# Layer 0 in three passes over the tokens: u first, then linear attention beside the state-space scan, then gates, half GLU and output projection

## The chip, the cores and the metric

The kernel runs on one core of a Trainium2 chip. The time is that of one launch in device microseconds (us). Profiled durations come from one execution that the hardware profiler recorded; engines are named as in the profile: PE (TensorE matmuls), PEld (its weight loads), DVE (VectorE), ACT (ScalarE), POOL (GpSimd), SP (SyncE, which issues the DMAs).

## What is computed

Two layers over a prompt of 4096 tokens of width 1024, and over a sample of 8 x 4 tokens that shares the weights. Layer 0 is the one that changes:

```
proj = rms_norm(x, g) @ w_in            # 1024 -> 512+512+256+256+512+16+512
u, gate_a, q, k, v, a_low, gate_b = split(proj)
y, s5_last = s5_scan(u, ...)            # 32 groups of 16 channels, one 64-dim complex diagonal state each, over all tokens
z = gelu(y); z = z * sigmoid(z @ w_glu + b_glu)          # half GLU
out_a = z * silu(gate_a)
log_a = log_sigmoid(a_low @ w_gate + b_gate) / 16
o, gla_last = gla_chunked(q, k, v, log_a, s0)            # 4 heads, chunks of 64
out_b = rms_norm(o, g) * silu(gate_b)
h = x + concat(out_a, out_b) @ w_out    # 1024 -> 1024
```

Layer 1 (projection, rotary, sliding-window attention with sinks, gate, projection) stays as it is.

## The kernel before

Tokens are taken in 16 windows of 256. Every product with a weight is made of three f16 matmuls (high by high, low by high, high by low parts), so x is first multiplied by its norm's factor (`x <- x,rb`, L312 on DVE), rounded (`xh`, L313 on ACT) and the rest taken (`xl`, L314 on POOL). Weights are split in the same way (L244, L245), each after a bound on its size was summed over its squares (`bound_all`, L212 on DVE).

Work is written as generators that yield costs. `merge` takes the next piece from the stream that is furthest behind its weight, and so sets the order of the instructions on each engine; every engine then runs its own list strictly in order.

`phase0` merges three streams. `ustream` projects u of window after window and writes it to DRAM. `s5stream` first builds the scan's tables for all 32 groups and then runs `s5win` as soon as u of four windows is there. `bounds` sums squares of weights. A unit of the scan is 4 groups by 1024 tokens, laid out as 128 positions of 8 tokens; there are 32 units, eight per call of `s5win`. A unit has 12 fp32 matmuls of 128x128 on PE (`pV`, L768; `pY`, L785 and L788), and between them on DVE a multiply (L773), a rotation (L746 to L750), four recurrences (L777), a multiply (L780), a second rotation, and two small copies (L779, L782). For the last eight units some of these operations are on POOL:

```
RO = ('vvvdv', 'vggdg')
merge((ustream(), 170.0), (s5stream(), SW), (bounds(), BW))
```

`phase1` runs window by window. `instream(w)` holds gate_a (`ga`), gate_b with the gate code (`gb`), q and k, v; `bstream(w)` holds the half GLU (`glu`), the chunked linear attention (`core`, whose first DVE operation in a window is `attm`, L1095) and the output projection (`outstream`, L1346 adds its result to x):

```
merge((bstream(w), 35.0), (instream(w + 1), 50.0), side)
```

The side stream holds the bounds of layer 1's weights in windows 0 to 6 and the sample in windows 7 to 9. The last eight units of the scan are run beside the loading of layer 0's weights, and layer 1's weights are loaded in the tail of `phase1`. Three PSUM banks (`pmm`) take the products of `phase1`.

`phase2` is layer 1.

Of the kernel before, what the change touches and what calls it, by code (L numbers as in the profile page):

```python
# [19 lines left out]
KT = 8  # L20
# [11 lines left out]
TW, SW, BW, HP, HS, HT, LW, SMP1 = 0.3, 100.0, 60.0, 100000, 0, 0, 27.0, 9  # L32
LW2 = 30.0
OB, WG = 2, 28
VQ = (0, 1)
GL, CA, CB = 0, 3.0, 40.0
# [3 lines left out]
EA, ST1 = 15, 12  # L40
RO = ('vvvdv', 'vggdg')
BW0 = 0
BE = 'v'
BG, SMP0, SC = 8.0, 7, 8.0
# [36 lines left out]


class Stage:


    def __init__(self, xp, og):
        self.xp, self.og, self.n = xp, og, 0

    def tile(self, shape, dtype, name):
        self.n += 1  # L90
        if self.n % 2:
            return self.xp.tile([128, 512], F32, name="x")
        a = self.og.tile([128, KT, NW], F16, name="ogh" if self.n % 4 else "ogl")
        return a.rearrange("p k n -> p (k n)").bitcast(F32)[:, 0:512]
# [12 lines left out]
class K:  # L107
# [87 lines left out]
    def bound_all(self, src, blocks, g, nk, name, sp, pp, tag="misc"):  # L195
# [3 lines left out]
        if g is not None and pp is not self.pms:  # L199
            g2 = sp.tile([128, nk], F32, name=name + "_g2")  # L200
            nc.vector.tensor_mul(g2, g, g)
        fr = self.cp.tile([128, len(ch) * nk], F32, name=name + "_fr")
        for i, (_, c, m) in enumerate(ch):
            for k in range(nk):
                st = sp.tile([128, 512], F32, name="wst")
                nc.sync.dma_start(st[:, 0:m], src[128 * k:128 * k + 128, c:c + m])
                a = fr[:, i * nk + k:i * nk + k + 1]
                if pp is self.pms or BE == "a":
                    nc.scalar.activation(st[:, 0:m], st[:, 0:m], AF.Square, bias=0.0,
                                     scale=g[:, k:k + 1] if g is not None else 1.0, accum_out=a)  # L210
                else:
                    (nc.vector if BE == "v" else nc.gpsimd).scalar_tensor_tensor(st[:, 0:m], st[:, 0:m], g2[:, k:k + 1] if g is not None else 1.0, st[:, 0:m],  # L212
                                     op0=OP.mult, op1=OP.mult, accum_out=a)
                yield 1.0
# [59 lines left out]
    def stats(self, acc, n, rst, blk0, wp, pp, tag="misc"):  # L274
# [7 lines left out]
        self.rms(ps, n, rst, blk0, wp)  # L282

    def rms(self, ps, n, rst, blk0, wp):
# [6 lines left out]
        nc.gpsimd.tensor_tensor(rst[0:m, blk0:blk0 + nb], v[0:m, 0:nb], self.mhalf[0:m, 0:nb], op=OP.pow)  # L291

# [12 lines left out]
    def xsplit(self, xs, n, rb, hp):  # L305
# [3 lines left out]
        for x in xs:  # L309
# [59 lines left out]
    def s5_tables(self):  # L369
        nc, I = self.nc, self.I  # L370
        with ExitStack() as e2:
            t = self.pool("s5t", es=e2)
            pp = self.pool("s5p", bufs=2, es=e2, space=PSUM)

            def T(name, *shape):
                return t.tile([128] + list(shape), F32, name=name)

            lam = T("lam", 2, G5)
            nc.sync.dma_start(lam, I["lam"])
            ld = t.tile([G5, 1], F32, name="ld")  # L380
            nc.sync.dma_start(ld, I["log_dt"])
            bc = T("bc", 4, G5, 16)
            nc.sync.dma_start(bc, I["s5_bc"])
            Dd = t.tile([16, G5], F32, name="Dd")
            nc.sync.dma_start(Dd, I["s5_d"])
            lre, lim = lam[:, 0], lam[:, 1]
            B1, B2, P1, P2 = (bc[:, k] for k in range(4))
            ec = T("ec", G5)
            nc.vector.memset(ec, math.e)
            for m in self.Mt:  # L390
                nc.gpsimd.memset(m, 0.0)
            yield 0.1

            dd = t.tile([G5, G5], F32, name="dd")
            nc.gpsimd.tensor_tensor(ld, ec[0:G5, 0:1], ld, op=OP.pow)
            nc.vector.tensor_scalar(dd, self.identf[0:G5, 0:G5], ld, None, op0=OP.mult)
            pd = pp.tile([128, 4, 128], F32, name="pv")
            nc.tensor.matmul(pd[:, 0, 0:G5], self.onesf[0:G5, :], dd, start=True, stop=True)
            dt = T("dt", G5)
            nc.vector.tensor_copy(dt, pd[:, 0, 0:G5])  # L400
            nc.vector.tensor_scalar(lim[0:64], lim[0:64], -1.0, None, op0=OP.mult)
            nc.vector.tensor_scalar(P1[64:128], P1[64:128], -1.0, None, op0=OP.mult)
            nc.vector.tensor_scalar(P2[64:128], P2[64:128], -1.0, None, op0=OP.mult)

            red = T("red", G5)
            nc.vector.tensor_mul(red, lre, dt)
            nc.vector.tensor_scalar(red[64:128], red[64:128], 8.0, None, op0=OP.mult)
            mg = T("mg", G5)
            nc.gpsimd.tensor_tensor(mg, ec, red, op=OP.pow)
            mag = T("mag", G5)  # L410
            for h in range(2):
                r = slice(64 * h, 64 * h + 64)
                nc.vector.tensor_copy(mag[r], mg[0:64])
                nc.vector.tensor_copy(self.r8[r], mg[64:128])

            ang = T("ang", 8, G5)
            nc.vector.tensor_mul(ang[:, 0], lim, dt)
            for j in range(1, 8):
                nc.vector.tensor_scalar(ang[:, j], ang[:, 0], 8.0 * 2.0**(j - 1), None, op0=OP.mult)
            kk = T("kk", 8, G5)  # L420
            nc.vector.tensor_scalar(kk, ang, 1.0 / TWO_PI, MAGIC, op0=OP.mult, op1=OP.add)
            nc.vector.tensor_scalar(kk, kk, MAGIC, None, op0=OP.subtract)
            for c in (C1, C2, C3):
                nc.vector.scalar_tensor_tensor(ang, kk, -c, ang, op0=OP.mult, op1=OP.add)
            nc.vector.tensor_scalar(ang, ang, 3.1415925, -3.1415925, op0=OP.min, op1=OP.max)
            sn, cs = T("sn", 8, G5), T("cs", 8, G5)
            nc.scalar.activation(sn, ang, AF.Sin, bias=0.0, scale=1.0)
            nc.scalar.activation(cs, ang, AF.Sin, bias=0.0, scale=0.5)
            nc.vector.tensor_mul(cs, cs, cs)
            nc.vector.tensor_scalar(cs, cs, -2.0, 1.0, op0=OP.mult, op1=OP.add)  # L430
            yield 1.0

            Lr, Li = self.Lr, self.Li
            nc.vector.memset(Lr[:, 0], 1.0)
            nc.vector.memset(Li[:, 0], 0.0)
            nc.vector.tensor_mul(Lr[:, 1], mag, cs[:, 0])
            nc.vector.tensor_mul(Li[:, 1], mag, sn[:, 0])

            def cmul(orr, oi, ar, ai, br, bi, tmp):
# [393 lines left out]
    def phase1(self, es0, tail):  # L833
# [572 lines left out]
        def some(g, n):  # L1406

            while n > 0:
                c = next(g, None)
                if c is None:  # L1410
                    return
# [738 lines left out]
```

## Time and profile before

| | us |
|---|---|
| three runs | 3288.75, 3296.31, 3296.82 (median 3296.31) |
| profiled execution | 3289.11, of which the span is 3287.3 |
| first u matmul to last u matmul | 14.5 to 403 |
| units of the scan | 195 to 502 |
| first `attm` of window 0, 1, 2 | 516.6, 623.1, 695.0 |
| first `attm` of windows 11 to 15 | 1457.5, 1537.6, 1617.8, 1698.0, 1769.0 |
| end of layer 0's last output projection, first product of layer 1 | 1822.0 |

The stretch up to 516.6 is called the head below, and the time from one window's first `attm` to the next window's a window interval. PE is busy for 3150.1 us, but a matmul's record lasts longer than the distance to the next one, so PE counts as busy while it waits between two of them for less than that.

### The profile page before, as it was taken

How to read it: one execution, taken by the hardware profiler on the slowest of the kernel's cores; microseconds unless marked ns; L12 is line 12 of the kernel's file. 1: busy time of each engine (PE TensorE's matmuls, PEld its weight loads, DVE VectorE, ACT ScalarE, POOL GpSimd, SP SyncE). 2: the span in 40 equal slices, each digit the busy share in tenths (PEclk: the TensorE clock that was granted, in tenths of full speed). 3: DMA queues.
4: the chain of work that ended last, by engine and by line, in shares of the span. 5: the costliest groups of instructions: out<-in, count | busy, mean ns of one | idle time of the engine just before them, and what ended most of it. 6: DMA issues, size and time to landing. Idle time of an engine off the chain costs nothing.

```text
span 3287.3 us, 68398 instructions
## 1 busy us (share of the span) xinstructions
PE 3150.1 (96%) x27293; PEld 2458.2 (75%) x27293; DVE 2054.4 (62%) x4785; ACT 1688.5 (51%) x4054; POOL 1261.2 (38%) x1292
## 2 busy tenths in 40 slices
PE   6898879899999999999999999999999999999999
PEld 5687766687788777788877667777777777777777
DVE  8869998644444443444446477666666666666675
ACT  4386556233344343343345366565555656555664
POOL 7824241211111211111111565554555555555552
PEclk9799989999999999999999999999999999999999
DMA  4297467411111112211113212111111111101111
GB/s 128 60 252 176 95 149 223 121 46 49 46 49 46 44 45 71 58 50 46 43 53 122 72 36 62 41 40 41 36 42 40 34 37 37 34 28 41 40 32 43
DMA packets 329521, 222.79 MB, mean 68 GB/s; under 512 B 142544, under 2 KB 302240, under 8 KB 329056
## 3 DMA queue, kind: packets, MB, share of 16 engines
q1 hardware_dynamic: 329200, 218.41, 24.2%
q8 instruction: 214, 3.51, 0.4%
q14 instruction: 107, 0.88, 0.1%
HBM read 164.94 MB, written 53.23 MB: 66 GB/s over the span
## 4 chain that ended last, share of the span: by engine, by line
PE 75%; DVE 11%; ACT 4%; issue 4%; DMA 4%; POOL 3%; SPq 1%; DVEq 0%; POOLq 0%; ACTq 0%
PE mm L325 13%; PE mm L326 13%; PE mm L327 13%; PE mm L334 7%; PE mm L335 7%; PE mm L336 7%; PE po L1760 3%; PE pt L1718 2%; PE ps L1699 2%; PE ps L1700 2%; PE pt L1568 1%; DVE z L777 1%; POOL xl L314 1%; DVE x L312 1%; DMA wst<-in_w_in 1%
## 5 line engine op out<-in xcount | busy, mean ns | idle before, releaser
L325 PE MATMUL mm<-ogh,woh 128*128 128x256 f16 x1472 | 401.3, 273 | 1.4 <-DVE xr L1346 1.4
L326 PE MATMUL mm<-ogl,woh 128*128 128x256 f16 x1472 | 401.3, 273 | 0.5 <-POOL ogl L1772 0.5
L327 PE MATMUL mm<-ogh,wol 128*128 128x256 f16 x1472 | 401.3, 273 | 0.0
L314 POOL TENSOR_TENSOR xl<-x,xh 128x512 f16<-128x512 f32 (+1 forms) x196 | 261.3, 1355 | 319.1 <-ACT xh L313 306.1
L1683 ACT ACTIVATE Sc<-Sc,ng,rq 128x128 f32<-128x128 f32 x512 | 245.6, 482 | 107.1 <-DVE ng L1677 105.7
L272 POOL TENSOR_TENSOR acc<-acc,sq 128x512 f32<-128x512 f32 x48 | 61.8, 1288 | 565.4 <-issue 370.4
L1711 POOL TENSOR_TENSOR Pl<-Sc,Ph 128x512 f16<-128x512 f32 x128 | 153.3, 1198 | 275.6 <-ACT Ph L1710 244.9
L326 PEld LDWEIGHTS <-woh 128*128 128x128 f16 x2112 | 207.2, 98 | 36.4 <-issue 9.8
L325 PEld LDWEIGHTS <-woh 128*128 128x128 f16 x2112 | 207.2, 98 | 31.6 <-issue 4.6
L336 PEld LDWEIGHTS <-xl 128*128 128x128 f16 x1536 | 151.0, 98 | 106.0 <-issue 6.7
L334 PEld LDWEIGHTS <-xh 128*128 128x128 f16 x1536 | 150.9, 98 | 102.5 <-issue 17.7
L327 PEld LDWEIGHTS <-wol 128*128 128x128 f16 x2112 | 207.1, 98 | 25.5 <-issue 3.1
L335 PEld LDWEIGHTS <-xh 128*128 128x128 f16 x1536 | 151.0, 98 | 84.0 <-issue 5.1
L325 PE MATMUL mm<-xh,wuh 128*128 128x256 f16 (+1 forms) x544 | 151.6, 283 | 14.2 <-ACT us L727 6.9
L313 ACT ACTIVATE xh<-x 128x512 f16<-128x512 f32 (+1 forms) x196 | 117.8, 618 | 75.6 <-DVE x L312 61.7
L326 PE MATMUL mm<-xl,wuh 128*128 128x256 f16 (+1 forms) x544 | 151.4, 284 | 4.9 <-POOL xl L314 4.9
L1720 ACT ACTIVATE PT<-pt 128x1024 f16<-128x1024 f16 x128 | 129.6, 1013 | 42.1 <-PE pt L1718 42.1
L327 PE MATMUL mm<-xh,wul 128*128 128x256 f16 (+1 forms) x544 | 151.1, 283 | 0.0
L312 DVE TENSOR_TENSOR x<-x,rb 128x512 f32<-128x512 f32 (+1 forms) x188 | 136.5, 781 | 22.5 <-ACT rb L302 18.2
L1346 DVE SCALAR_TENSOR_TENSOR xr<-mm,soa,xr 128x512 f32<-128x512 f32 x64 | 47.7, 745 | 160.5 <-PE mm L327 155.8
L326 PE MATMUL mm<-xl,wi1gah 128*128 128x256 f16 x512 | 141.4, 277 | 3.0 <-POOL xl L314 3.0
L327 PE MATMUL mm<-xh,wi1gal 128*128 128x256 f16 x512 | 141.0, 276 | 2.4 <-DVE wi1gal L245 2.4
(730 smaller groups left out, 10558.9 us busy)
## 6 DMA issues: line engine op xcount, KB each, us to landing
x<-in_xT SPq DMA_DIRECT2D x128, 256.0 KB
wst<-in_w_in SPq DMA_DIRECT2D x64, 256.0 KB
xr<-in_xT SPq DMA_DIRECT2D x64, 256.0 KB
h_d<-xr SPq DMA_DIRECT2D x64, 256.0 KB
x<-h_d SPq DMA_DIRECT2D x64, 256.0 KB
xr<-h_d SPq DMA_DIRECT2D x64, 256.0 KB
out_yT<-xr SPq DMA_DIRECT2D x64, 256.0 KB
wst<-in_w_out SPq DMA_DIRECT2D x48, 256.0 KB
```

The lines of the kernel that those rows point to most:

```text
L312: nc.vector.tensor_mul(x, x, rb[:, None, :].to_broadcast([128, 2, n]))
L313: nc.scalar.activation(h, x, AF.Copy, bias=0.0, scale=1.0)
L314: nc.gpsimd.tensor_sub(l, x, h)
L325: nc.tensor.matmul(ps, wh[:, k0 + k, c], xh[k], start=(k == 0), stop=False)
L326: nc.tensor.matmul(ps, wh[:, k0 + k, c], xl[k], start=False, stop=False)
L327: nc.tensor.matmul(ps, wl[:, k0 + k, c], xh[k], start=False, stop=(k == n - 1))
L334: nc.tensor.matmul(ps, xh[k][:, t], wh[:, k, c0:c1], start=(k == 0), stop=False)
L335: nc.tensor.matmul(ps, xh[k][:, t], wl[:, k, c0:c1], start=False, stop=False)
L336: nc.tensor.matmul(ps, xl[k][:, t], wh[:, k, c0:c1], start=False, stop=(k == n - 1))
L1683: nc.scalar.activation(Sc[:, i], Sc[:, i], AF.Exp, bias=ng[:, i:i + 1], scale=scale[:, i:i + 1], accum_out=de[:, i:i + 1])
L1711: nc.gpsimd.tensor_sub(Pl, Sc, Ph)
L1720: nc.scalar.activation(PT, pt.rearrange("p a i n -> p (a i) n"), AF.Copy, bias=0.0, scale=1.0)
```

## The change

Layer 0 is cut into three passes over all tokens, with weights and tables placed to suit.

- Pass A (`phaseA`): u of all 16 windows; the scan's tables for the first two of eight quarters (4 groups each); bounds and splits of the weights of gate_b, q, k and v.
- Pass B (`phaseB`): window by window gate_b, v, q and k of the next window beside the linear attention of this one, and beside them the scan (`some(s, SB)`: pieces of a total weight of 10 per window). The scan goes quarter by quarter, with four units to a quarter, and the tables of quarter q+2 are built after quarter q in one of two buffers. All of a unit's multiplies are on DVE. When the scan is done, the same stream loads the weights of gate_a, half GLU and output. The side stream holds bounds in windows 0 to 6 and the sample in 7 to 9, as before. The norm's factor comes by a broadcast DMA from DRAM (`rbload`) and not by a matmul; the multiply x by rb is on POOL. The halves of x and of the attention's output are written to DRAM.
- Pass C (`phaseC`): the halves come back from DRAM; gate_a and half GLU of the next window beside the output projection of this one, and beside them the splits of layer 1's weights.

Passes A and B have two PSUM banks for products, pass C three. Matmuls on PE go from 25,975 to 25,976; DMAs that SP issues from 1,197 to 1,778.

```
-RO = ('vvvdv', 'vggdg')
+SB, BG, SC = 10.0, 13.0, 8.0
+RO = ("vvvdv", "vvvdv", "vvvdv", "vvvdv")
...
     def xsplit(self, xs, n, rb, hp, mul=None, dst=None):
...
-            nc.vector.tensor_mul(x, x, rb[:, None, :].to_broadcast([128, 2, n]))
+            (mul or nc.vector).tensor_mul(x, x, rb[:, None, :].to_broadcast([128, 2, n]))
             nc.scalar.activation(h, x, AF.Copy, bias=0.0, scale=1.0)
             nc.gpsimd.tensor_sub(l, x, h)
+            if dst is not None:
+                for i, a in enumerate((h, l)):
+                    nc.sync.dma_start(dst[:, i, 2 * c:2 * c + 2], a)
...
+        for q in range(8):                       # s5_units
+            for w in range(4):
+                yield from unit(q, w)            # yields 1.7 and 0.9
+            if q + 2 < 8:
+                yield from self.quarter(q + 2)   # yields 3 x 0.7, 0.5, 1.5, 0.5
...
-        merge((ustream(), 170.0), (s5stream(), SW), (bounds(), BW))
+        merge((ustream(), 170.0), (tables(), 18.0), (loads(), 66.0))     # end of phaseA
...
+        def prep(w):                             # phaseB
+            rb = self.rbload(self.rs0[w], Pb)
+            Ws[w]["x"] = self.xsplit(Ws[w]["x"], n, rb, hp, nc.gpsimd, self.xp_d[w])
...
+        merge((instream(0), 50.0), (self.some(s, SB), SB))
+        for w in range(NWIN):
...
+            merge((core(w), 35.0), (instream(w + 1) if w + 1 < NWIN else None, 50.0), (self.some(s, SB), SB), side)
...
+        run(front(0))                            # phaseC; front = gate_a, half_glu
...
+        for w in range(NWIN - 1):
+            merge((outstream(w), 21.0), (front(w + 1), 17.0), (self.some(wg, 3.0), 3.0),
+                  (self.some(smp, 4.0) if w < 4 else None, 4.0))
```

How the order on two engines moves, at the places that the prediction speaks of. First DVE while u is projected. Before, between the multiplies of one window's x and the next, stand operations of the scan (`X`, `t`, `z`, `carry`):

```order
L780 TENSOR_TENSOR X<-z,CT_109 128x4x128
L743 TENSOR_TENSOR t_3119<-z,ST_110 64x512
L744 TENSOR_TENSOR t_3119<-z,ST_110 64x512
L748 TENSOR_TENSOR t_3841<-t_3841,ST_86 128x512
L773 TENSOR_TENSOR X<-pV,CT_85 128x4x128
L779 COPY X<-carry 128x4
L750 TENSOR_TENSOR X<-X,t_3119 128x4x128
L750 TENSOR_TENSOR X<-X,t_3841 128x4x128
L220 COPY wa_n_4447<-misc 128x1
L312 TENSOR_TENSOR x<-x,rb 128x512 x4
L782 COPY carry<-X 128x4
```

In the change the same multiplies (now at L299) have only the sums of squares between them, once the two quarters' tables are built:

```order
L299 TENSOR_TENSOR x<-x,rb 128x512 x4
L274 TENSOR_SCALAR var<-pt 128x2
L734 TENSOR_TENSOR sq<-sq 128x512
L299 TENSOR_TENSOR x<-x,rb 128x512 x4
L734 TENSOR_TENSOR sq<-sq 128x512
L274 TENSOR_SCALAR var<-pt 128x2
L734 TENSOR_TENSOR sq<-sq 128x512 x2
L299 TENSOR_TENSOR x<-x,rb 128x512 x4
```

The scan's operations have left this stage. They stand in pass B; this is DVE there in the change, in the window in which the sample begins, where `q` and `k` are what empties the banks of products (`mm`) and `X`, `t`, `z` and `carry` are one unit of the scan:

```order
L603 TENSOR_TENSOR X<-X,t_9927 128x4x128
L625 SCALAR_TENSOR_TENSOR z<-r_95,carry,X 128x128 x4
L628 TENSOR_TENSOR X<-z,CT_85 128x4x128
L601 TENSOR_TENSOR t_9927<-z,ST_86 64x512
L602 TENSOR_TENSOR t_9927<-z,ST_86 64x512
L603 TENSOR_TENSOR X<-X,t_9927 128x4x128
L630 COPY carry<-X 128x4
L627 COPY X<-carry 128x4
L943 SCALAR_TENSOR_TENSOR q_10015<-mm,sr_3602,E 128x256
L948 SCALAR_TENSOR_TENSOR k_10016<-mm,sr,E 128x256
```

Here the operations that free a PSUM bank have moved behind most of a unit. Last, POOL in windows after the sample. Before, it held the rests of x (`xl`), the squares of the output (`acc`) and the rest of the half GLU's output (`ol`):

```order
L314 TENSOR_TENSOR xl<-x,xh 128x512 x4
L272 TENSOR_TENSOR acc<-acc,sq 128x512
L277 TENSOR_TENSOR acc<-acc 128x256
L291 TENSOR_TENSOR rst_77<-var,mhalf 128x2
L1058 TENSOR_TENSOR ol<-A,oh 128x512 x2
```

In pass B of the change it holds the multiplies of x, between the rests of x and the head norm's powers (`rs`):

```order
L301 TENSOR_TENSOR xl<-x,xh 128x512 x4
L299 TENSOR_TENSOR x<-x,rb 128x512 x3
L965 TENSOR_TENSOR rs<-ss,mhalf 128x4
L299 TENSOR_TENSOR x<-x,rb 128x512
L965 TENSOR_TENSOR rs<-ss,mhalf 128x4
L301 TENSOR_TENSOR xl<-x,xh 128x512 x4
```

The multiplies have come over from DVE, and the squares and the half GLU have gone to pass C.

## Rows read from the trace of the kernel before

**Rows 1.** The profile page: span, busy time of each engine, DVE in 40 slices.

```profile
span 3287.3 us, 68398 instructions
PE 3150.1 (96%) x27293; PEld 2458.2 (75%) x27293; DVE 2054.4 (62%) x4785; ACT 1688.5 (51%) x4054; POOL 1261.2 (38%) x1292
DVE  8869998644444443444446477666666666666675
```

**Rows 2.** Five stretches: us, busy PE, PEld, DVE, ACT, POOL; clock, DMA share, GB/s.

```profile
0.00:516.60 516.60, 418.63 (x3243) 356.85 (x3244) 458.01 (x893) 306.05 (x621) 253.87 (x187) 0.90 0.58 146
516.60:695.00 178.40, 165.35 (x1321) 130.19 (x1321) 119.56 (x322) 73.62 (x165) 30.33 (x28) 0.97 0.47 141
695.00:1768.90 1073.90, 1066.21 (x8906) 842.50 (x8905) 475.24 (x1217) 430.31 (x1009) 200.21 (x174) 1.00 0.19 52
1768.90:1822.00 53.10, 47.55 (x389) 38.99 (x387) 39.74 (x92) 25.64 (x56) 17.24 (x18) 0.90 0.53 161
1822.00:3287.00 1465.00, 1452.33 (x13442) 1089.69 (x13439) 961.81 (x2264) 852.88 (x2205) 759.54 (x888) 1.00 0.13 39
```

**Rows 3.** Stretches inside the head, columns of rows 2.

```profile
14.50:166.90 152.40, 121.29 (x884) 99.96 (x884) 133.55 (x256) 59.67 (x112) 127.13 (x88) 0.80 0.31 77
166.90:189.20 22.30, 22.30 (x201) 19.78 (x199) 6.63 (x10) 16.92 (x38) 7.31 (x7) 0.97 0.98 255
202.00:403.00 201.00, 175.36 (x1472) 156.51 (x1470) 196.96 (x377) 130.52 (x273) 59.60 (x43) 0.95 0.67 165
195.00:490.00 295.00, 246.57 (x1985) 218.84 (x1986) 286.62 (x538) 187.19 (x388) 100.61 (x72) 0.92 0.66 161
```

**Rows 4.** DVE by line, 195 to 517 us: first and last of the scan's nine groups.

```profile
L777 DVE TENSOR_TENSOR_SCAN z<-r,carry,X 128x128 f32<-128x128 f32 x128 | 62.0, 545 | 0.1
...
L779 DVE COPY X<-carry 128x4 f32<-128x4 f32 x31 | 8.9, 291 | 0.0
```

**Rows 5.** Tables on DVE, 0 to 517 us: first and last of thirteen groups.

```profile
L511 DVE SCALAR_TENSOR_TENSOR Ks<-identf,Dd,Ks 16x16 f32<-16x16 f32 x32 | 13.3, 464 | 0.0
...
L524 DVE TENSOR_TENSOR CT<-CT,cs 128x256 f32<-128x256 f32 x4 | 1.5, 404 | 0.0
```

**Rows 6.** POOL by line, 0 to 517 us.

```profile
L314 POOL TENSOR_TENSOR xl<-x,xh 128x512 f16<-128x512 f32 x71 | 105.2, 1503 | 106.1 <-ACT xh L313 105.9
...
L780 POOL TENSOR_TENSOR X<-z,CT 128x512 f32<-128x512 f32 x8 | 11.2, 1402 | 21.3 <-DVE z L777 18.4 <-DVE wi_gs L238 2.9
```

**Rows 7.** Lines L777, L312 and L314 over the span: ns min/median/max.

```profile
L777 DVE TENSOR_TENSOR_SCAN z<-r,carry,X x128: 448/460/1366, 206.7 to 493.6; 128x128 f32<-128x128 f32 x128
L312 DVE TENSOR_TENSOR x<-x,rb x188: 205/686/1755, 15.3 to 3137.4; 128x512 f32<-128x512 f32 x184, 128x64 f32<-128x64 f32 x4
L314 POOL TENSOR_TENSOR xl<-x,xh x196: 305/1171/4447, 19.7 to 3139.7; 128x512 f16<-128x512 f32 x192, 128x64 f16<-128x64 f32 x4
```

**Rows 8.** Four fp32 matmuls in the timeline (two records each), then an f16 one.

```profile
433.21 1.06 PE L785 MATMUL pY<-U,Mt 128*128 128x128 f32 x8
434.10 0.27 PE L327 MATMUL mm<-xh,wi1gal 128*128 128x256 f16 x1
```

**Rows 9.** One window interval without sample or scan, columns of rows 2.

```profile
1537.60:1617.80 80.20, 80.20 (x667) 64.41 (x665) 35.03 (x86) 31.46 (x74) 15.55 (x14) 1.00 0.18 47
```

**Rows 10.** DVE by line in that interval: one of its groups.

```profile
L1346 DVE SCALAR_TENSOR_TENSOR xr<-mm,sob,xr 128x512 f32<-128x512 f32 x5 | 3.7, 746 | 9.6 <-PE mm L327 9.6
```

**Rows 11.** The three window intervals that hold the sample, columns of rows 2.

```profile
1168.80:1264.00 95.20, 91.17 (x762) 68.48 (x763) 45.21 (x123) 41.03 (x100) 15.93 (x14) 0.98 0.16 42
1264.00:1374.80 110.80, 108.72 (x918) 81.64 (x920) 43.16 (x121) 37.59 (x91) 19.87 (x17) 1.00 0.24 67
1374.80:1457.50 82.70, 82.70 (x699) 66.12 (x692) 33.81 (x90) 32.32 (x75) 15.00 (x15) 1.00 0.19 50
```

**Rows 12.** Chain that ended last: one DMA wait after the head.

```profile
541.76 4.53 DMA wst<-in_w_in
```

**Rows 13.** SP's timeline: one DMA issue.

```profile
1457.56 0.37 SPq L1358 DMA_DIRECT2D h_d<-xr  x1
```

More of the change, by code (lines that the diff above doesn't have):

```diff
@@ new lines, in ustream, with loads, tables @@
+                                nc.sync.dma_start(self.u_d[w][ct][:, :, 64 * (h // 2):64 * (h // 2) + 64], us[:, ct])
+        def loads():
+            yield lambda: self.udone >= 0
+            yield from self.bound_all(I["w_in0"], self.B_IN0, self.g0, KT, "wi1", bp, pms, "pt", ("v", "a"))
+            self.wr["wi1"] = self.pow2(self.bound["wi1"], "wi1")
+            for b in ("v", "gb", "qk"):
+                yield from self.load_w(I["w_in0"], self.SRC[b], self.g0, "wi1", *W1[b], bp)
+        def tables():
+            yield from self.s5_tables()
+            yield from self.quarter(0)
+            yield from self.quarter(1)
@@ L946, in instream @@
             x = W["x"]
-            if w + 1 < NWIN:
-                yield from gate_a(w)
             alT = Pa.tile([16, NW], F32, name="alT")
@@ new lines, in phaseB @@
+        Ws = [{} for _ in range(NWIN)]
+        Ws[0]["x"] = self.xload(xp, I["xT"], 0, n)
+        prep(0)
+        s, bnd, smp = s5(), bounds(), sample()
+        merge((instream(0), 50.0), (self.some(s, SB), SB))
+        for w in range(NWIN):
+            side = (None, 1.0)
+            if w < SMP0:
+                side = (self.some(bnd, BG), BG)
+            elif SMP0 <= w <= SMP1:
+                if w == SMP0:
+                    run(bnd)
+                    eb.close()
+                    self.smp = self.pool("smp1", es=eb, side=R)
+                side = (self.some(smp, SC), SC)
+            merge((core(w), 35.0), (instream(w + 1) if w + 1 < NWIN else None, 50.0), (self.some(s, SB), SB), side)
+            if w == SMP1:
+                run(smp)
+                eb.close()
+            Ws[w] = None
@@ L1406, in some @@
[L1406 to L1411, printed above, removed]
-                yield c
-                n -= 0 if callable(c) else c
-        bnd, smp = bounds(), sample()
-        for w in range(NWIN - 1):
-            side = (None, 1.0)
-            if BW0 <= w < SMP0:
-                side = (some(bnd, BG), BG)
-            elif SMP0 <= w <= SMP1:
-                if w == SMP0:
-                    run(bnd)
-                    eb.close()
-                    self.smp = self.pool("smp1", es=eb)
-                side = (some(smp, SC), SC)
-            merge((bstream(w), 35.0), (instream(w + 1), 50.0), side)
-            if w == SMP1:
+        Ws = [{} for _ in range(NWIN)]
@@ L1454, in weights @@
-        def weights():
-            for b, (c, m) in src.items():
-                yield from self.load_w(I["w_in1"], [(0, c, m)], self.g1, "wi2", *W2[b], st)
-        st = Stage(xp, og2)
-        wg = weights()
-        for _ in range(WG):
-            next(wg)
-        rb = self.rbcast(self.rst1, 0, NW, xp, self.pta, tag="pt", rtag="x")
+        er, el = self.er2, ExitStack()
+        W2 = self.W2
+        hp = self.pool("h2", bufs=4, es=er, side="right")
+        xp = self.pool("x2", bufs=3, es=er, side="right")
```

1202 lines of the change are left out of this document (594 added, 608 removed).

## The prediction

> **What bounds the kernel now.** I read the page first. PE is busy for 96% of the span, so by the average it is the bound; but DVE's slices stand at 8 and 9 in the first six of forty and at 4 in the next eleven [rows 1]. So the stages are looked at apart. Layer 1 is 1465.0 us with PE busy for 1452.3, and the thirteen window intervals from 695 on have PE busy for 1066.2 of 1073.9 [rows 2]: there the change can gain little but by leaving out matmuls, and it leaves out none. In the head DVE is busy for 458.0 of 516.6 us [rows 2], and in the scan, from 195 to 490, for 286.6 of 295.0 while PE shows 246.6 of records that count waits too [rows 3]. That PE waits there is seen in the u projection: where nothing else presses, two windows of u take 22.3 us, all of it PE [rows 3], 11.15 a window; from 202 to 403, with the scan beside, the rest of u goes at about 21 a window with DVE at 197.0 of 201.0 [rows 3]. The head is therefore DVE's, the rest PE's. What lies idle there is DVE: 35.0 of 80.2 us in a plain window interval [rows 9].
>
> **Prices of PE's work.** The 22.3 us hold 201 matmuls [rows 3]: 0.111 each for 128x256 in f16. Four fp32 ones take 0.89 from one row's start to the next [rows 8], 0.223 each; a unit of the scan has 12, so 2.67 us. Gate_a, half GLU and output have 96 + 48 + 192 = 336 matmuls a window, 37.3 us; the plain interval of 80.2 [rows 9] leaves 42.9 for gate_b, v, q, k and the attention. The three intervals with the sample show PE busy for 91.2, 108.7 and 82.7 [rows 11], 42 over three plain ones.
>
> **Pass A, the head up to the first attention.** What leaves it: 28 of 32 units. The first instream runs with 10 of scan beside it, and a unit yields 2.6, so four units start there. PE's work in the new head is 16 x 11.15 = 178.4 for u, 42.9 for the first instream, 10.7 for four units, and some 30 for norm sums, table matmuls of two quarters and bounds (an estimate without a row of its own): 262. DVE loses 28/32 of the scan's nine groups, which sum to 229.6 [rows 4], so 200.9, and 6/8 of the tables' thirteen, which sum to 66.3 [rows 5], so 49.7; 458.0 becomes 207, below PE. How well PE is fed is bounded by two stretches: 121.3 of 152.4 (0.80) where the tables are built beside u, and 22.3 of 22.3 after them [rows 3]. With the start at 14.5 these give 14.5 + 262/0.80 = 342 and 14.5 + 262 = 277. I take 0.86, as two quarters are built in place of eight, and so **319 in place of 516.6**.
>
> **Pass B, ten intervals with the scan.** The remaining 28 units and six quarters of tables (4.6 of yield each) make 28 x 2.6 + 6 x 4.6 = 100: ten windows at 10. PE: 10 x 42.9 = 429, 28 x 2.67 = 74.8, six quarters with eight fp32 matmuls 10.7, and the sample 42, which I count whole here though part of it goes to pass C: 556.5, or 55.7 an interval. DVE per interval: from 35.0 go eight output operations at 0.746 [rows 10], the twelve of half GLU and gate_a at about the same, and four x multiplies at the median of 0.686 [rows 7], which leaves 17.3. A unit is (229.6 + 24 x 0.686)/32 = 7.7, since 24 operations of its size (16 of L750, 8 of L780 [rows 6]) come back from POOL; 2.8 units are 21.6, tables 5.0, the half of thirteen bound blocks that falls on DVE 5: 49 us, 87% of PE's 55.7. So PE stays the bound, but with little to spare. What is lost on it over 55.7 has no row at this share of DVE. The low end is nothing, as in plain intervals at 44%. The next intervals, 516.6 to 695.0, lost 18 over two plain ones with DVE at 119.6 of 178.4 [rows 2], but there the chain stands on DMAs of weights, such as 4.53 at once [rows 12]. The high end is 14 an interval (first rival). I take 6, a tenth: **616**.
>
> **Five intervals without scan**: 5 x 42.9 = 214.5. In these PE has little else after q and k, while x of the next window must be rounded and its rest taken on ACT and POOL; between 0 and 8 each, I take 3: **230**.
>
> **Pass C and layer 1.** 16 x 37.3 = 597, and 1465.0 as before [rows 2]. The last stretch of layer 0 before lost about 16 of its 53.1 us over the 37.3 of products [rows 2]; the last attention and the first gate_a now each stand with little beside them, so 16 and 10 more for reading back the halves: 26. Sum: **2088**.
>
> **What I cost at nothing.** The multiply x by rb frees DVE of 64 x 0.686 = 44 us and gives POOL 64 x 1.40, the price of the nearest POOL row (L780) [rows 6]; a window's share, 5.6, lies in a POOL that is busy for 15.6 of 80.2 [rows 9], a window ahead. In POOL's list the head norm's powers stand behind three such multiplies, 4 us, for which the attention waits; gate_b and v matmuls cover that, and without them it costs 4 a window. The 581 more DMAs at 0.37 an issue [rows 13] are 215 us of SP over the whole run. The halves of x are 1 MB a window; at the 255 GB/s that 166.9 to 189.2 moved [rows 3] this is 4 us per window if not covered, and 47 GB/s move in a plain one [rows 9]. On SP scan output, u for the next unit and x stand in one line; a write that waits for its gelu holds the loads behind it, and x, a window ahead, is the last to feel it.
>
> **Sum.** 319 + 616 + 230 + 2088 = 3253, and 1.8 around the span (3289.11 less 3287.3): 3255 against 3289.1 profiled. The median of the runs is 7.2 above the profiled one, so 3262 against 3296.3, 1.0% less. A difference of 0.3%, 10 us, is about what can be told from no change: 3286 and 3306.
>
> **Rivals.** First, slower: *the banks wait behind the scan*. In DVE's list of pass B, q and k, which empty PE's banks, stand behind most of a unit. A unit is 7.7 on DVE; PE fills a bank of 24 matmuls in 2.7 and has two, not three. If every unit holds PE for the difference, 5, then 2.8 units cost 14 an interval: 70 in place of 62, 10 x 8 = 80 more, **3342**. For it speaks 87% on DVE and that PE waited in the scan before; against it, that DVE was at 97% there and here has 7 us to spare. It decides at 34/10 above 62: from 65.1 an interval on the kernel is slower.
>
> Second, *DVE and POOL get into each other's way*. The recurrence takes 460 ns at the median and up to 1366, x's multiply 686 and up to 1755 [rows 7], and POOL's rest of x 1171 at the median [rows 7] but 1503 on average in the head [rows 6]. If DVE can't run while POOL does its four multiplies at 1.40 and four rests at 1.17, 10.3 us, DVE needs 49 + 10.3 = 59.3 an interval; with 6 lost 65.3, so 36 more in ten: **3298**, no change. Against it: from 14.5 to 166.9 DVE's 133.6 and POOL's 127.1 lay in 152.4 us [rows 3], so much of both runs side by side. The Trainium skill (GPSIMD Engine Reference, 1. Specifications) says that GpSimd's SBUF interfaces are shared with VectorE, with contention where a DVE instruction has two SBUF inputs, and in its opening that ordinary elementwise work is the wrong thing for it. By that rule this rival would hold in full; the long records agree with it, the side-by-side stretch only in part.
>
> Third, *DVE's idle time takes all of the scan*: the head at 287 (277 and 10 of handover) and 1 lost an interval: 32 + 50 less, **3180**. Plain intervals and layer 1, with DVE at 961.8 of 1465.0 and PE full [rows 2], speak for it.
>
> **How the numbers follow.** The forecast has 0.52; its own range is 3225 to 3300 (head 277 to 342, four to nine lost an interval), with 0.07 of the 0.52 within 0.3%. The first rival has 0.18, the second 0.10 (0.07 within 0.3%, 0.03 above), the third 0.20. So faster 0.45 + 0.20 = 0.65, same 0.14, slower 0.21. The range leaves out the outer parts of the first and third rival, a tenth each: 3185 to 3335.
>
> **What would show it.** The first attention's `attm` near 319 and u at about 13 a window; ten intervals near 62, then five near 46; DVE busy for 45 to 60 in the first ten; scan recurrences spread from the head to the tenth interval; pass C near 37 a window. I am wrong if the head stays above 345, if PE in those intervals waits for `q`, `k` or `gb` on DVE for more than 9 each, or if POOL's multiplies grow well over 1.4 and DVE's with them.

## The result, and the profile after

The changed kernel takes 3530.76 us (median of four runs, 3520.21 to 3537.08) against 3296.57 (four runs of the kernel before): 1.0707 times as long, with a 95% interval of 1.067 to 1.0744. The profiled execution took 3531.23, with a span of 3529.4.

The page of the changed kernel, for [rows 1]: span, busy times, then PE, DVE and the granted clock in 40 slices.

```profile
span 3529.4 us, 69759 instructions
PE 3245.0 (92%) x27358; PEld 2513.2 (71%) x27358; DVE 1984.0 (56%) x4803; ACT 1700.7 (48%) x4045; POOL 1250.2 (35%) x1363
PE   5778789899897998899999999999999999999999
DVE  6441676676665333543333338766666666666666
PEclk9888889899897989999999999999999999999999
```

DVE is no longer full anywhere in the first third, as meant. But PE isn't full there either, and its clock stands below nine tenths in nine of the first fifteen slices. By stretch, in the columns of [rows 2]: u; the way to the first attention; ten intervals with the scan; five without; the start of pass C; the rest of it; layer 1.

```profile
14.50:349.60 335.10, 250.81 (x1999) 212.50 (x2000) 157.35 (x338) 149.75 (x266) 132.61 (x127) 0.88 0.60 119
349.60:427.40 77.80, 53.03 (x355) 38.68 (x354) 49.23 (x118) 40.53 (x92) 23.17 (x18) 0.84 0.69 203
427.40:1130.90 703.50, 624.48 (x4384) 459.39 (x4383) 477.97 (x1297) 369.96 (x871) 163.66 (x157) 0.90 0.36 99
1130.90:1383.10 252.20, 238.49 (x1626) 168.46 (x1627) 86.91 (x300) 90.06 (x266) 46.80 (x41) 0.91 0.14 45
1383.10:1500.00 116.90, 93.72 (x785) 73.95 (x786) 63.95 (x131) 52.54 (x105) 14.76 (x14) 0.93 0.57 155
1500.00:2048.90 548.90, 529.47 (x4797) 470.44 (x4795) 200.20 (x307) 145.89 (x231) 114.12 (x107) 0.98 0.39 108
2048.90:3529.40 1480.50, 1453.32 (x13412) 1088.51 (x13409) 944.46 (x2290) 842.25 (x2190) 752.21 (x890) 0.99 0.14 41
```

Term by term, measured against predicted: head 427.4 for 319 (+108); ten intervals 703.5 for 616 (+88); five 252.2 for 230 (+22); from the last attention on 2146.3 for 2088 (+58, of which pass C 43 and layer 1 15). Together 276, the distance from 3253 to 3529. Against the kernel before, the head did get 89 shorter; all that follows it takes 331 longer (3102.0 for 2770.7).

What PE's list stands on in pass A is a chain. The waits by engine, 14 to 427 us (who waited for whom: us, times, longest):

```profile
POOL xl L301 <- ACT xh L300: 154.3, 19, 23.6
ACT sq L730 <- DMA x<-in_xT: 98.5, 36, 8.7
DVE sq L734 <- ACT sq L730: 91.8, 22, 14.0
PE pt L737 <- DVE sq L734: 42.3, 12, 9.9
```

And three pieces of the chain that ended last, between 140 and 200 us (start, us, what):

```profile
157.29 9.89 DMA x<-in_xT
...
174.14 10.49 DMA x<-in_xT
...
197.27 10.10 DMA x<-in_xT
```

PE waits for the sums of squares, DVE for the squares, ACT for x, and the chain stands some 10 us on a load of x about once in each window of u. That is a round of waits, with no engine full. Two stretches of u show what it costs, nine windows (the fifth to the thirteenth) and then the last three, behind which nothing is left to load or to square:

```profile
132.40:320.20 187.80, 143.87 (x1105) 121.84 (x1106) 67.64 (x118) 85.65 (x142) 56.34 (x51) 0.84 0.55 104
320.20:351.30 31.10, 31.04 (x285) 27.79 (x282) 4.18 (x7) 9.69 (x11) 6.40 (x8) 1.00 0.27 53
```

The nine take 20.9 each, of which 4.9 are idle time of PE and 3.3 the lower clock (0.16 x 20.9); the three take 10.4 each, all of it PE at full clock.

One plain interval of pass B, for [rows 9], first by the stretch and then in PE's timeline:

```profile
1183.00:1234.10 51.10, 48.10 (x327) 33.94 (x325) 18.48 (x61) 18.29 (x54) 11.53 (x10) 0.90 0.17 55
```

```profile
1191.75 0.99 PE L975 MATMUL pt<-identf,og 128*128 128x128 f32 x3 [2.15 <-DVE og L969]
...
1198.09 0.43 PE L326 MATMUL mm<-wi1gbh,xl 128*128 128x264 f16 x1
1198.31 0.43 PE L324 MATMUL mm<-wi1gbh,xh 128*128 128x264 f16 x1
...
1203.66 0.28 PE L325 MATMUL mm<-wi1gbl,xh 128*128 128x264 f16 x1
1203.77 0.28 PE L326 MATMUL mm<-wi1gbh,xl 128*128 128x264 f16 x1
```

PE waits 2.15 us in the attention and works through its small fp32 matmuls; the wide ones of gate_b that follow start 0.22 us apart at 1198 and 0.11 apart at 1203. A mean clock of 0.90 over 51.1 us means that 0.10 x 2 x 51.1 = 10 us of it were at the lower level of 1.2 GHz. In [rows 2] the clock stands at 1.00 from 695 to 1769.

The last of the ten intervals holds no scan any more (its last recurrence starts at 1033.1), but the end of the sample and the loads of pass C's weights:

```profile
1049.00:1130.90 81.90, 59.30 (x387) 38.91 (x386) 42.56 (x112) 38.10 (x91) 12.69 (x11) 0.77 0.59 178
```

It takes 31.5 more than a plain one of 50.4, with PE idle for 22.6 us and another 18.8 lost to the clock (0.23 x 81.9).

### The profile page after: what moved, and what is told of

Same layout as the page of the kernel before. It is cut to its first block, busy times and chain, and to the rows that moved or that the text cites. A ratio compares the mean times of both kernels' runs of the same rounds, so it can differ in the third digit from the quotient of the medians.

```text
span 3529.4 us, 69759 instructions
## 1 busy us (share of the span) xinstructions
PE 3245.0 (92%) x27358; PEld 2513.2 (71%) x27358; DVE 1984.0 (56%) x4803; ACT 1700.7 (48%) x4045; POOL 1250.2 (35%) x1363
## 4 chain that ended last, share of the span: by engine, by line
PE 63%; DVE 11%; DMA 11%; issue 5%; ACT 5%; POOL 3%; SPq 1%; ACTq 0%; DVEq 0%; POOLq 0%
PE mm L315 12%; PE mm L316 11%; PE mm L317 11%; PE mm L324 5%; PE mm L325 5%; PE mm L326 5%; DMA wst<-in_w_in 3%; DMA x<-in_xT 3%; PE po L1779 3%; POOL xl L301 2%; PE pt L1737 1%; PE ps L1719 1%; PE ps L1718 1%; DVE z L625 1%; DMA x<-h_d 1%
## 5 line engine op out<-in xcount | busy, mean ns | idle before, releaser
L301 POOL TENSOR_TENSOR xl<-x,xh 128x512 f16<-128x512 f32 (+1 forms) x196 | 237.4, 1233 | 543.2 <-ACT xh L300 540.9
L315 PE MATMUL mm<-ogh,woh 128*128 128x256 f16 x960 | 261.8, 273 | 7.0 <-DVE xr L1823 4.2
L316 PE MATMUL mm<-ogl,woh 128*128 128x256 f16 x960 | 261.8, 273 | 0.0
L317 PE MATMUL mm<-ogh,wol 128*128 128x256 f16 x960 | 261.8, 273 | 0.0
L324 PEld LDWEIGHTS <-xh 128*128 128x128 f16 x1536 | 156.7, 102 | 115.7 <-issue 19.2
L325 PEld LDWEIGHTS <-xh 128*128 128x128 f16 x1536 | 155.8, 101 | 105.6 <-issue 19.1
L324 PE MATMUL mm<-wi1gbh,xh 128*128 128x264 f16 x512 | 155.7, 305 | 12.1 <-ACT sc L947 5.0
L315 PE MATMUL mm<-oh,woh 128*128 128x256 f16 x512 | 141.3, 276 | 21.2 <-DVE xr L1352 19.5
L326 PE MATMUL mm<-wi1gbh,xl 128*128 128x264 f16 x512 | 154.1, 303 | 2.9 <-POOL xl L301 2.8
L325 PE MATMUL mm<-wi1gbl,xh 128*128 128x264 f16 x512 | 155.1, 304 | 0.0
```

The costliest lines, as they stand in the source:

```text
L315: nc.tensor.matmul(ps, wh[:, k0 + k, c], xh[k], start=(k == 0), stop=False)
L316: nc.tensor.matmul(ps, wh[:, k0 + k, c], xl[k], start=False, stop=False)
L317: nc.tensor.matmul(ps, wl[:, k0 + k, c], xh[k], start=False, stop=(k == n - 1))
L324: nc.tensor.matmul(ps, xh[k][:, t], wh[:, k, c0:c1], start=(k == 0), stop=False)
L325: nc.tensor.matmul(ps, xh[k][:, t], wl[:, k, c0:c1], start=False, stop=False)
L326: nc.tensor.matmul(ps, xl[k][:, t], wh[:, k, c0:c1], start=False, stop=(k == n - 1))
```

## The experiments

Each kernel is the changed one with the edit shown. Times in the table are taken from each profile: last u matmul, first `attm`, ten intervals, five intervals, pass C up to layer 1's first product, span (us). Each experiment ran once; the change's own four runs spread over 17 us. Where only pass A was edited, the ten intervals still move between 691.7 and 709.2, the five between 248.4 and 252.9 and pass C between 655.5 and 669.7, as the whole order is planned anew; differences below that are not read. The section on the kernel before lets `merge` set the order on each engine. That is not all of it: a planner behind it moves instructions once more, and two of the edits below (b_serial, c_late) didn't move what they were meant to move.

| | last u | first attm | ten | five | pass C | span |
|---|---|---|---|---|---|---|
| the change | 349.6 | 427.4 | 703.5 | 252.2 | 665.8 | 3529.4 |
| a_x12 | 316.0 | 395.0 | 691.7 | 252.3 | 669.7 | 3492.7 |
| a_q | 340.4 | 424.3 | 699.8 | 252.5 | 656.7 | 3513.1 |
| a_all | 333.3 | 418.8 | 700.1 | 248.4 | 656.3 | 3505.9 |
| a_norm | 312.8 | 394.4 | 702.2 | 251.6 | 663.1 | 3488.9 |
| a_nob | 346.2 | 424.7 | 709.2 | 251.7 | 662.5 | 3534.3 |
| a_xq | 339.8 | 421.4 | 695.9 | 252.9 | 659.7 | 3513.4 |
| a_us2 | 350.0 | 433.4 | 696.7 | 252.5 | 655.5 | 3521.3 |
| a_us2xq | 331.9 | 414.7 | 692.1 | 252.3 | 660.2 | 3503.1 |
| a_h12 | 328.1 | 408.4 | 694.4 | 251.3 | 659.5 | 3494.6 |
| a_fillhalf | 419.6 | 501.6 | 698.1 | 252.8 | 659.2 | 3595.1 |
| b_q | 342.1 | 427.8 | 719.8 | 253.3 | 659.3 | 3543.7 |
| b_dve | 340.6 | 413.1 | 691.6 | 252.4 | 668.7 | 3505.7 |
| b_core12 | 348.6 | 426.2 | 793.5 | 296.2 | 658.2 | 3653.1 |
| b_serial | 352.6 | 437.0 | 721.3 | 251.4 | 665.5 | 3560.4 |
| b_fillhalf | 348.8 | 435.1 | 708.3 | 260.1 | 661.4 | 3542.4 |
| b_fill | 352.9 | 456.0 | 747.1 | 281.5 | 657.9 | 3621.8 |
| c_late | 350.4 | 427.3 | 703.1 | 248.2 | 668.4 | 3529.1 |
| best | 315.8 | 391.8 | 718.7 | 253.3 | 672.5 | 3519.4 |

**Pass A: what sets u's pace.** First the tiles, and the lines that DMAs stand in.

```
a_x12:  -xp = self.pool("x0", bufs=8, ...)   +xp = self.pool("x0", bufs=12, ...)
a_q:    ud writes: -nc.sync +nc.scalar;  rs0 writes: -nc.sync +nc.gpsimd
a_all:  both, and xload of window i+1 issued in stage(i) in place of stage(i+1)
```

> Pass A has 12 tiles for x in place of 8, so three windows of x can be under way and not two. Theory 1 (u's pace of about 20 us a window, with DVE busy under half of the time, is set by the round of x: load, squares, norm, split, tile free again, over two windows of tiles): the round of about 38 us is then shared by three, u comes at 13 to 15 a window, its last matmul near 270 in place of 349.6, and the first attm near 350 in place of 427.4; the span falls by 60 to 90. Rival 1 (the loads of x are late because they stand on SP behind writes of u and of the norm's factors, which wait for ACT and POOL): more tiles don't shorten a line, u stays at 18 or more, the last matmul after 320. Rival 2 (the halves of x, of which there are still two windows' worth, hold it): no change.

> In pass A the writes of the norm's factors are issued by POOL and the writes of u by ACT, each right behind the instruction that makes the data, so that on SP only loads stand in line. Rival 1 (SP's line): the 45 us of SP waiting for us and the 18 for rst go, loads come earlier, u at 14 to 17 a window, last u matmul at 260 to 310, span 40 to 80 less. Theory 1 (round of x over two windows of tiles): u stays at 18 to 20 and the last matmul after 330; the span changes by less than 15.

> Pass A with 12 tiles for x, writes of u on ACT and of the norm's factors on POOL, and each window of x loaded one window earlier than before. What 12 tiles alone gave was 32 us in the head, the other queues alone 3. If u's pace is set by how late x lands (PE's norm sums stand in front of u's matmuls in its list and wait for squares, squares wait for x, about 10 us from issue to landing), the load is now out of the way: u at 11 to 14 a window, its last matmul before 270 and the first attm before 350. If it is set by DVE, ACT and POOL doing squares, splits of weights and tables in one order, u stays at 16 or more and the last matmul after 300, with PE waiting for xh, xl or sq and not for x.

12 tiles gave 34 us in u, two fifths of what theory 1 asked for (80); the other queues gave 9, and both with an earlier load less than the tiles alone. So the line on SP isn't it, and the round over x's tiles is a part only. Next the work in the round.

```
a_norm: 12 tiles; -8 matmuls of [128x1] a window for the norm   +sq summed on DVE first, 2 matmuls
a_nob:  12 tiles; -yield from self.bound_all(... "wi1" ...)   +self.wr["wi1"] = (w, r)
```

> Pass A with 12 tiles for x, and with the norm's squares summed on DVE before PE sums over partitions (as the kernel before did it for windows 6 to 15): 2 norm matmuls a window in place of 8, two more additions on DVE. In the change every one of these matmuls stands in PE's list ahead of u's and takes about 0.23 at full and 0.47 at half clock. If this is what u's window has over 10.5 to 11.15 (6 x 0.23 to 0.47 is 1.4 to 2.8, and fewer waits of PE for sq), the last u matmul comes at 280 to 295 against 316.0 with 12 tiles alone, and the first attm at 355 to 375 against 395.0. If u's pace is the round of x (load, squares, norm, split), it stays within 8 of 316.

> Pass A with 12 tiles for x, and without the bounds of layer 0's weights: 32 weight loads of up to 256 KB and their squares on DVE and ACT are left out, and the weights are scaled by the bound of u's part. If the side work beside u (loads in x's DMA queue, squares that wait for weights in ACT's and DVE's lists) makes u slow, the last u matmul comes at 270 or earlier against 316.0 with 12 tiles alone, by more than the 32 x 0.7 = 22 us that the squares take on two engines. If u's own round is the limit, it moves by less than 12.

Neither moved u forward: 312.8 against 316.0, and 346.2 with less work. Neither the norm's matmuls nor the bounds are what slows u; the splits of weights beside it stayed in both. Leaving the bounds out even cost what the tiles had given, with the clock at 0.82 from 60 to 310 us where a_x12 has 0.89; why, these runs don't show. Then x's loads and u's writes.

```
a_xq:    12 tiles; x's loads in stage(): -nc.sync +nc.gpsimd
a_us2:   9 tiles;  us = wp.tile(..., name="us", bufs=1 -> 2)
a_us2xq: a_us2, with x's loads as in a_xq
```

> Pass A with 12 tiles for x, and the loads of x from window 1 on issued by POOL, whose xl is what frees a tile, so that they neither stand in SP's line nor in its queue behind weights and u. If x's landing is what PE's list waits for (squares waited 57 us for x with 12 tiles), u's last matmul comes at 260 to 290 against 316.0. If the issue on POOL costs as much as it saves, 305 to 330.

> Pass A with a second tile for two windows of u on their way to DRAM, and 9 tiles for x in place of 8; x's loads stay on SP. If the write of u with one tile is a limit by itself, the last u matmul comes at 300 to 325 against 349.6; if x's round is the first limit and u's write only the next, 335 to 350.

> The same with x's loads on POOL. If x's landing and u's write together set u's pace, one taking over where the other is mended, both mended give 12 to 15 a window: the last u matmul at 250 to 290 and the first attm at 330 to 370. If it stays over 325, the pace has a third cause that these runs don't show.

With x loaded from POOL, the squares' wait for x from 40 to 345 us fell from 57.3 us (a_x12) to 24.7, and u came later, at 339.8 for 316.0. The chain of a_xq between 130 and 180 us shows what took over, the write of u out of its one tile:

```profile
136.85 11.76 DMA ud<-us
...
168.34 9.14 DMA ud<-us
```

A second tile for it, alone, changes nothing; both edits together, with 9 tiles for x, give 18 us in place of 60 or more. By what was expected of a_us2xq, u's pace then has a third cause. Last, more work for PE in the same places, and the tiles of x's halves.

```
a_fillhalf: 12 tiles; mmB(ps[:, k], wuh, wul, ...) issued twice for k = 0
a_h12:      -hp = self.pool("h0", bufs=8, ...)   +hp = self.pool("h0", bufs=12, ...)
```

> Pass A with 12 tiles for x, and half of u's matmuls issued twice (the second time the bank is started anew): 48 more a window, 48 x 0.111 = 5.3 us of PE at full clock, 85 in all. If waits between engines set u's pace, the added work lies in PE's idle time and lifts the clock: the last u matmul moves from 316.0 to 316 to 345 and the low stretches in the head shrink. If PE's own work sets it, it moves by 85 or more, to 400.

> Pass A with 12 tiles each for the high and low halves of x and the 8 tiles for x of the change. If the round that sets u's pace closes over the halves (PE reads them, then ACT and POOL may write the window after next, then x's tile is free and the next load begins), three windows of halves let PE run ahead: the last u matmul at 260 to 300 in place of 349.6. If it closes over x's own tiles, as the 32 us with 12 of those say, it stays at 335 to 350.

The 85 us of added matmuls moved the last one by 104. The expectation put such a move down to PE's own work; but PE idles for 53 of u's 301.5 us without them (a_x12) and for 60 of 405.1 with them (a_fillhalf):

```profile
14.50:316.00 301.50, 248.45 (x1993) 210.48 (x1993) 169.45 (x337) 147.71 (x266) 137.10 (x127) 0.91 0.64 131
14.50:419.60 405.10, 344.90 (x2761) 295.87 (x2761) 168.19 (x335) 152.10 (x266) 132.05 (x127) 0.88 0.50 98
```

So PE's work and the waits add up, they don't lie side by side. That is what a round does in which PE has a place: PE reads the halves, then ACT and POOL may write the next ones, then x's tile is free, then x is loaded. A third window of halves gave 21, a third window of x 34; no run has both. Nor was a rival tried: the norm's matmuls for a later window stand in PE's list among u's, and PE waits there for the squares (42.3 us), so that their place in the list may set the pace as much as the tiles do.

**Pass B: what an interval costs.**

```
b_q:   xsplit's stores: -nc.sync +nc.scalar (high), nc.gpsimd (low); ob_d's stores: -nc.sync +nc.scalar
b_dve: xsplit(..., nc.gpsimd, self.xp_d[w])  ->  xsplit(..., None, self.xp_d[w])
```

> In pass B the writes of the halves of x are issued by ACT (high) and POOL (low), and those of the attention's output by ACT, and no longer by SP. Theory 2 (in pass B the loads of x, of the norm's factor and of u stand on SP behind writes that wait for xh and ogl, so x is late, POOL's list stands still with the head norm's powers in it, and PE waits and drops to the lower clock): SP's waits in the five intervals without scan, 185 us on ACT, vanish, these intervals fall from 51 to 43 to 47, and the ten with scan from 70.4 to 63 to 67; the span is 60 to 100 less. Rival (DVE's list holds PE back: units of the scan ahead of what empties the banks): the five fall a little, the ten stay at 69 or more; less than 30 in all.

> The multiply of x by its norm's factor in pass B is back on DVE, as before the change. If POOL's list (multiplies that wait for a load, with the head norm's powers behind them) is what delays the attention, the five intervals without scan fall from 51 to about 46, and the ten with scan keep at 68 to 71, since DVE gets 2.8 us more each. If DVE is what binds the ten, they grow to 72 or more. If the loads themselves are late whatever engine multiplies, the five stay at 50 to 52, with DVE waiting for x in place of POOL.

Both left the five intervals at 252 to 253. Theory 2 falls: SP did stand still for 185 us there, and nobody needed it. In the ten intervals b_q came to 719.8, 16 more than the change, and b_dve to 691.6, 12 less. The latter is within what the order alone moves, so no price of the multiply on POOL can be read from it.

```
b_core12:   merge((core(w), 35.0 -> 12.0), (instream(w + 1), 50.0), ...)
b_fill:     mmA(ps[:, 0:264], *W1["gb"], ...) issued twice
b_fillhalf: the same for i == 0 only
```

> In pass B the attention's weight in the merge goes from 35 to 12, which spreads its small fp32 matmuls over all of the next window's products in place of its first half. Theory 3 (the miss in the five intervals without scan is the granted clock: one stretch of 10.24 us at 0.5 in each, right after PE has worked through the attention's small matmuls with gaps, costs 5 us an interval; PE's idle time itself is as predicted): with wide matmuls between the small ones the low stretches go, the five intervals fall from 50.4 to 43 to 46 with a mean clock over 0.97, and the ten fall by 3 to 6 each. Rival (the attention's own chain from q and k to the output sets the interval, and any order of PE meets it): the five stay at 49 to 54 or grow, whatever the clock does.

> In pass B every matmul of gate_b is issued twice (the second pass starts its bank anew, so the result stays): 96 more wide matmuls a window, 96 x 0.113 = 10.8 us of PE at full clock, about what gate_a was in these windows before the change. Theory 3 (a plain interval is 50.4 and not 42.9, since the attention's small matmuls and their waits, which gate_a, half GLU and output covered before, now stand nearly bare: about 3 us of idle and a stretch of 10.24 us at half clock): the added work takes the place of idle time and of the low clock, the five intervals grow by 1 to 6 only, to 51 to 56, with a mean clock over 0.95. Rival (PE is simply full at its clock, the 7.5 us are work that I counted wrong): they grow by 10 to 12, to 61 to 63, at the same clock of 0.91.

> The same for one of the two halves of each block of gate_b: 48 more wide matmuls a window, 5.4 us. Theory 3: the five intervals grow by 0 to 3, and what the first half costs is less than or equal to what the second costs. Rival: 5 to 6 more.

The five intervals of b_fillhalf, b_fill and b_core12, in the columns of [rows 2]:

```profile
1143.40:1403.50 260.10, 249.72 (x1867) 183.14 (x1868) 83.87 (x300) 89.90 (x266) 46.72 (x41) 0.96 0.15 47
```

```profile
1203.10:1484.60 281.50, 273.83 (x2108) 205.48 (x2109) 88.67 (x301) 90.89 (x266) 46.84 (x41) 0.99 0.13 40
```

```profile
1219.70:1515.90 296.20, 234.74 (x1591) 161.89 (x1590) 86.77 (x301) 88.88 (x266) 46.76 (x41) 0.84 0.13 39
```

The first 5.4 us of added wide matmuls cost 1.6 an interval in the five (7.9 in all), with the clock at 0.96 where it was 0.91; the ten moved by 4.8 in all, too little to be read, with the clock at 0.95 for 0.90. The second 5.4 cost 4.3 in the five and 3.9 in the ten: in the five the clock is at 0.99 by then and there is little left to fill. So in a plain interval some 4 us of the 5.4 were to be had for nothing. Of these, 2.5 are lower clock (0.09 x 252.2 against 0.04 x 260.1, over five) and 0.7 idle time.

Spreading the attention over the interval did the opposite of what theory 3 expected: PE idles for 296.2 - 234.7 = 61.5 us in place of 13.7, and the clock falls to 0.84. PE's longest waits in the five intervals of b_core12:

```profile
PE pa L988 <- DVE og L969: 28.7, 5, 8.3
PE pt L1016 <- ACT og L961: 13.1, 4, 3.5
```

Once in each interval the attention's next block (`pa`, L988) waits up to 8.3 us until the output of the block before it (`og`) has been made from the same bank; in the change `pa` waits for 1.2 us in all five. It isn't enough that wide matmuls stand somewhere between the small ones. This is the rival of that expectation: the attention's own chain sets the interval.

```
b_serial: +run(self.some(s, 110.75)) ahead of instream(0); the stream s again from window 7 on
```

> All 32 units of the scan and their tables run alone at the start of pass B, before the first instream; the ten windows hold no scan, and the loads of gate_a's, half GLU's and the output's weights start at window 7. This measures what the scan costs beside the attention (703.5 less ten plain intervals of 50.4 is about 200) and what it costs alone. By DVE's durations alone it is 32 x 7.0 to 7.7 and tables 50, so 270 to 300 in the head. If the ten intervals then come to 50 to 53, plus 30 for the sample, the scan beside the attention was nearly the price of its DVE time and little was hidden; the kernel is then 30 to 100 slower than the change. If they stay over 60, it isn't the scan that holds them but bounds, sample and clock.

This didn't measure what it was meant to: the planner spread the scan all the same, four units ahead of the first attention and 28 over the six intervals behind it, its recurrences running to 890.9 in place of 1033.1. It does give the price of the rest: windows 7 to 9, with sample, loads of pass C's weights and no scan, take 194.5, 43 over three plain ones of 50.4, where I took 42 for the sample. What is left of the ten is 703.5 - 504 - 43 = 156, or 5.4 us for each of the 29 units that they hold, with its share of tables and bounds and of what the loads cost more where they all come in the tenth interval.

**Pass C, and the three together.**

```
c_late: (self.some(wg, 3.0), 3.0)  ->  (self.some(wg, 3.4) if w >= 2 else None, 3.0)
best:   a_norm and b_dve together
```

> In pass C the splits of layer 1's weights begin two windows later, at a weight of 3.4 a window and no longer 3. If the 23 us that PE idles between 1383 and 1500, and the lower clock behind it, come from the order of ACT and DVE in which splits that wait for weights stand ahead of what empties PE's banks, pass C (665.8 from the last attm of B to the first product of layer 1) falls by 15 to 25. If they come from reading back x, z and the attention's output at the start, with nothing beside, less than 8.

> The three edits that helped or may help together: 12 tiles for x, the norm's sums on DVE, and in pass B the multiply of x on DVE. By the single ones (32, 20 to 30, 23 less) the span is 3440 to 3460; with the plain intervals at 50 and pass C at 666 untouched it stays over 3400, slower than before by 4 to 5%. Under 3400 would say that the pieces hang together more than I think.

Pass C came to 668.4 with c_late. That says nothing of the splits of layer 1's weights, which the edit did not move: from 1379 to 1500 us ACT has 35 of the 40 in both kernels. So whether they make pass C's 43 us is not shown. The three edits together gave 10 of the 70 to 90 hoped for: the head kept its gain and the ten intervals lost 15. No version came near the kernel before.

## Why the prediction was wrong

**The head** (predicted 319, measured 427.4). The step that failed: "That PE waits there is seen in the u projection", with 11.15 a window as what u takes when DVE lets it. PE's work was priced well: 335.1 us of u hold 84 of idle time and 40 of lost clock (0.12 x 335), which leaves 211 where my sum had 208. But those two windows at 11.15 were a burst out of stock: POOL had written the last halves of x for them at 136.7 and 169.2 us, while PE was at matmuls of tables. The change has such a burst at its end, three windows at 10.4. With DVE busy for 157 of 335 us, u still took about 20 a window. Taking the scan away uncovered a second limit at nearly the same pace, the round of x between SP, ACT, DVE, POOL and PE. That x's and its halves' tiles have a part in it is shown by a_x12 and a_h12, and that PE's work adds to the waits by a_fillhalf; what would bring it to 11 is not shown. My feed of 0.86 came from two stretches in which tables or a full stock of x set the pace; it was 0.62. The first attention then came 78 us after u, where 53.6 at 0.86 gave 62.

**The ten intervals** (616, measured 703.5). PE's work was right again: 556.5, plus 703.5 - 624.5 = 79 idle, plus 0.10 x 703.5 = 70 lost to the clock, is 705.5. DVE was right: 47.8 an interval for 49. POOL's multiplies took 1.36 for 1.40. What failed is the 6 lost in each interval ("I take 6, a tenth"), and the term under it: "the plain interval of 80.2 [rows 9] leaves 42.9". I subtracted gate_a, half GLU and output as work and didn't ask what they covered. The five intervals without scan show it bare: 50.4, not 42.9, of which 2.7 is idle time, as I took it to be, and 4.5 the clock (0.09 x 252.2 / 5), which I had left out everywhere. That gate_a, half GLU and output had been cover and not only work is what b_fillhalf shows: 5.4 us of wide matmuls put back cost 1.6. Over 55.7 of work the ten lose 14.7 an interval in place of 6. Plain ones lose 7.5 of that, too, and the 7.2 left are near the 6 that I had for the scan. The tenth interval alone loses 41 of the 149 that are idle time or clock; the sum has no term for the loads of pass C's weights that it holds.

**The rivals.** The first gave 70 an interval, and 70.4 was measured, but by another mechanism: its wait, PE at banks that DVE empties too late, is not among PE's longest (for `gb` and `k` on DVE it is 1.2 us in all ten, for `q` none). The waits of PE in the ten intervals begin:

```profile
PE pt L975 <- DVE og L969: 11.0, 7, 3.0
PE pY L635 <- DVE X L603: 10.0, 7, 4.4
PE pt L975 <- DVE p L969: 6.1, 1, 6.1
```

They are the attention's own chain, the scan's second product and the sample, a few us each. That wide matmuls could be added nearly free decides nothing here, as waits for full banks would have hidden them, too. The second rival, DVE and POOL in each other's way, asks for 36 in the ten intervals and is not borne out as a price: with the multiply back on DVE (b_dve) they came 12 shorter, which can't be told from a change of order, and the five the same. The rule of the Trainium skill (GPSIMD Engine Reference, 1. Specifications) beside it may still hold; no run here isolates it. The third needed DVE's spare time to be all that was missing, which the five intervals contradict: they lose 7.5 each with DVE busy for 86.9 of 252.2 us. The forecast's own range, 3225 to 3300, is narrower than its two terms make it together (3200 to 3315); the measured time lies far outside either.

**From the last attention on** (2088, measured 2146). Pass C idles for 43 us and loses 19 to the clock (0.07 x 116.9 + 0.02 x 548.9). Its start and its first windows, with the sample beside, hold half of that. Which term of mine (the 16, the 10, or the 37.3 a window with layer 1's splits beside it) was short is open, as c_late moved nothing. Of layer 1's 15 us, 7 are idle time of PE in its first 51 us (8.8 for 2.0); the rest is open.

**What I costed at nothing.** SP's 581 more DMAs and their waits were nothing in the five intervals of pass B (b_q). The read and write of x's halves didn't show up as a bound. The norm's sums, which the change does with 8 matmuls a window in place of 2 from window 6 on, I overlooked; in a_norm, with 2 again, u's last matmul comes 3 us earlier.

## What to carry to other kernels

Work that is taken out of a dense stretch takes its cover along: price what stays not by subtraction, but by what its own chain of small steps takes with nothing beside it, the lower clock included. A pace seen for two windows may be a stock running out, not a rate; before a bound is lifted, follow one window's round through all engines and tiles, since the next limit may stand right behind. And where idle time and lower clock come together, a few us of useful wide matmuls in that place cost little, which speaks for leaving such a product (here gate_a) beside the chain that it covers. Last, an edit of an order is worth reading only after the trace shows that the order moved: here two of three in passes B and C left in place what they were to move.

## What the runs showed of the hardware that I had not expected

TensorE's clock fell once in each plain interval of pass B, to 1.2 GHz for 7 to 10 us, while PE was at the attention's small fp32 matmuls, with single waits of 3.0 us at most; with 5.4 us of wide matmuls added, the mean clock of the five intervals was 0.96 in place of 0.91, with 10.8 it was 0.99. And the chain of a_xq stood 9 and 12 us on writes of 256 KB in runs of 256 bytes (`ud`), about as long as that of the change on loads of x of that size, 10 us.
